# Strided attention on one core: moving the buffers of all transfers to multiples of 256 bytes in SBUF

## The chip, the cores and the metric

The kernel runs on one core of a Trainium2 chip. A core has a matrix engine (TensorE, PE in the profile), a vector engine (VectorE, DVE), an activation engine (ScalarE, ACT), a general engine (GpSimd, POOL) and a sync engine (SyncE, SP) that here does nothing but issue transfers. Sixteen DMA engines move data between the main memory (HBM) and the core's own memory (SBUF). SBUF has 128 partitions, and a tile takes the same range of bytes in each of them, so that a tile has one start address. PSUM is the small memory that TensorE writes. The metric is the time of one execution in microseconds; the kernel before takes 129.6 us (median of three runs, 129.14 to 129.7).

## The reference

Every query position attends to the same 16 key positions, those at multiples of 64. All data are float32; 8 batches times 12 heads make 96 heads of 1024 positions by 64 values.

```python
batch, heads, seq, dim = (8, 12, 1024, 64)      # stride 64
attend_positions = np.arange(0, seq, stride)
for i in range(seq):
    scores = np.einsum('bhqd,bhkd->bhqk', q, k) * scale     # k: K at the attended positions
    weights = np.exp(scores - np.max(scores, axis=-1, keepdims=True))
    weights = weights / (np.sum(weights, axis=-1, keepdims=True) + 1e-10)
    result[:, :, i, :] = np.einsum('bhqk,bhkd->bhqd', weights, v)[:, :, 0, :]
```

All of Q is read (25.2 MB) and all of the result written (25.2 MB); of K and V only 16 rows of each head are read, 0.4 MB each.

## The kernel before

The 96 heads are worked on in 24 groups of four, g = 0 to 23. A group's Q is 1 MB: one transfer loads it into one of ten buffers qn (QBUFS, lines 71 and 85), 8192 bytes in each partition. A group's result is 1 MB as well: it is gathered in one of eight buffers out_sb (OBUFS, lines 72 and 87) and one transfer stores it. K and V come at the start, each in one transfer of 256-byte rows, into k_raw and v_raw (lines 83, 84, 103 and 105).

For each group, `cast` (line 191) turns the loaded Q into bf16, one half on POOL and one on ACT; `transpose` (line 203) turns it on DVE; `scores` (line 213) multiplies it with the keys on PE in four matmuls into PSUM, and ACT takes the exponential; `values` (line 181) spreads the group's values on POOL; `outputs` (line 239) multiplies the weights with the values on PE, with the sums of the weights as further columns. DVE takes the reciprocals and scales two of the three parts of the result; ACT copies the third to SBUF and POOL scales it. `store` (line 265) writes the group out.

All transfers are issued on SP's queue by `_copy` (line 24), K and V by the queue's ordinary call. The order is written out by hand (line 80 switches the scheduler off): K, the first Q load, V and nine more Q loads at the start; then, in the loop over g from line 300, the steps ahead for later groups, the outputs of g, the store of g and the load of g + 10. The first two Q loads have rows of 8192 bytes on the side of the main memory (n = 128 in line 97), the others rows of 32768 bytes, each of which fills four partitions. A store reads 8192 bytes of each partition and writes them as two rows of 4096 bytes (line 269).

Every tile of the pool const (line 74) has its own place in SBUF, one behind the other in the order of the calls of const.tile. 16 KB and four small constants of 32 bytes each come first in SBUF, so the first tile, k_raw, begins at byte 16512. The two tiles that the change moves are identity (line 110, 256 bytes in each partition), from which the masks and the permutation are built at the start, and k_bf (line 141, 1536 bytes), the keys as bf16.

Of the kernel before, what the change touches and what calls it, by code (L numbers as in the profile page):

```python
# [10 lines left out]
FP32 = mybir.dt.float32  # L11
BF16 = mybir.dt.bfloat16
# [36 lines left out]
def kernel(  # L49
# [10 lines left out]
    B, H, S, D = Q.shape  # L60
# [3 lines left out]
    P = 128  # L64
    HG = 4
    NG = B * H // HG
    NC = NG // 2
# [6 lines left out]
    const = ctx.enter_context(tc.tile_pool(name="const", bufs=1))  # L74
# [5 lines left out]
    ctx.enter_context(tc.manual_schedule())  # L80


    k_raw = const.tile([P, NC, D], FP32, name="k_raw")
    v_raw = const.tile([P, NC, D], FP32, name="v_raw")
    qn_bufs = [const.tile([P, 32 * D], FP32, name=f"qn{i}") for i in range(QBUFS)]
    qb_bufs = [const.tile([P, 32 * D], BF16, name=f"qb{i}") for i in range(2)]
    out_bufs = [const.tile([P, 4, 8, D], FP32, name=f"out_sb{i}") for i in range(OBUFS)]
# [19 lines left out]
        load(g)  # L107


    identity = const.tile([P, P], BF16, name="identity")  # L110
    s_sel = const.tile([P, 4], BF16, name="s_sel")
    mask = const.tile([P, 4, D], BF16, name="mask")
    perm_v = const.tile([P, 2, 2, 2, 2, NK], BF16, name="perm_v")
# [24 lines left out]
    nc.gpsimd.tensor_copy(out=v_all[:, :, 4 * D :], in_=s_sel.unsqueeze(1).to_broadcast([P, 3, 4]))  # L138
    nc.gpsimd.tensor_copy(out=mask, in_=s_sel.unsqueeze(2).to_broadcast([P, 4, D]))

    k_bf = const.tile([P, NC, D], BF16, name="k_bf")
    k_r = const.tile([P, NC, D], BF16, name="k_r")
    v_bf = const.tile([P, NC, D], BF16, name="v_bf")
    v_rep = const.tile([P, NC, 2, D], BF16, name="v_rep")
# [205 lines left out]
```

## Time and profile before

| | |
|---|---|
| median of three runs | 129.6 us (129.14 to 129.7) |
| profiled execution | 129.29 us, its span 127.2 us |
| DVE, ACT, POOL, PE busy | 85.3, 84.6, 78.0, 62.8 us |
| data moved by DMA | 51.19 MB, mean 403 GB/s |
| Q loads, stores | 24 and 24 of 1 MB, median 14.5 and 14.4 us from issue to landing |

The span runs from the first to the last instruction of one profiled execution; the time of the execution has some 2 us more around it. Busy time is the sum of an engine's instructions. The page of the profile also cuts the span in 40 slices and gives the share of each in which an engine, and the 16 DMA engines on average, were busy. A packet is the piece in which a DMA engine moves data; the trace records the start, the length and the size of each.

### The profile page before, as it was taken

The page shows a single profiled execution, that of the slowest core. Times are in us where ns is not written, and L with a number is a line of the kernel's source. Part 1 is how long each engine was busy: PE and PEld are TensorE (multiplying, and loading weights), DVE is VectorE, ACT ScalarE, POOL GpSimd, SP SyncE. Part 2 cuts the span into 40 slices and gives each one's busy share as a digit, 9 for nine tenths or more (in the row PEclk, how much of TensorE's full clock was granted, in tenths as well). Part 3 has the DMA queues.
Part 4 walks back from the last instruction along what each step waited for, and adds up shares of the span by engine and source line. Part 5 has one row for each costly group of instructions (what it writes and reads, how often), then busy time and mean ns, then how long its engine had stood idle before and what let it go on. Part 6 is the DMA issues. An engine that isn't in the chain of part 4 may idle for free.

```text
span 127.2 us, 1113 instructions
## 1 busy us (share of the span) xinstructions
PE 62.8 (49%) x292; PEld 29.6 (23%) x292; DVE 85.3 (67%) x151; ACT 84.6 (66%) x111; POOL 78.0 (61%) x89
## 2 busy tenths in 40 slices
PE   0005259374656666667666646366777656420000
PEld 0001023132322332322333323133433323100000
DVE  5921385459967996796979799797987976730000
ACT  4171905968799989977897979979787895420000
POOL 4082365918567956897696997969689693451000
PEclk9999999959997799855999999999756999955555
DMA  2999999898998989999999989999999899999991
GB/s 65 360 320 492 423 402 454 371 474 340 505 407 369 513 348 417 461 379 438 461 384 443 477 363 469 430 387 492 402 387 484 363 420 430 425 420 430 425 410 59
DMA packets 7910, 51.19 MB, mean 403 GB/s; under 512 B 3872, under 2 KB 3872, under 8 KB 3872
## 3 DMA queue, kind: packets, MB, share of 16 engines
q1 hardware_dynamic: 7904, 51.12, 97.0%
q8 instruction: 2, 0.03, 0.1%
q14 instruction: 4, 0.03, 0.1%
HBM read 25.95 MB, written 25.17 MB: 402 GB/s over the span
## 4 chain that ended last, share of the span: by engine, by line
DVE 30%; POOL 18%; PE 15%; ACT 14%; DMA 7%; issue 4%; SPq 1%; POOLq 1%; DVEq 0%
DVE out_sb L256 15%; DVE qt L205 9%; POOL out_sb L259 8%; DMA qn<-in_Q_dram 7%; PE sc L218 7%; PE o_ps L246 6%; ACT out_sb L258 6%; POOL qb L195 5%; DVE rec L254 5%; POOL v_all L183 3%; ACT w_all L230 3%; ACT qb L196 2%; PE o_ps L170 1%; POOLq L345 1%; ACT k_t L158 1%
## 5 line engine op out<-in xcount | busy, mean ns | idle before, releaser
L246 PE MATMUL o_ps<-v_all,w_all 128*128 128x260 bf16 x192 | 37.0, 309 | 37.2 <-DVE out_sb L256 31.3
L259 POOL TENSOR_TENSOR out_sb<-out_sb,rec 128x768 f32<-128x768 f32 x24 | 35.3, 1471 | 27.2 <-ACT out_sb L258 27.2
L256 DVE TENSOR_TENSOR out_sb<-o_ps,rec 128x768 f32<-128x768 f32 (+1 forms) x48 | 39.6, 825 | 1.6
L230 ACT ACTIVATE w_all<-sc 64x512 bf16<-64x512 f32 x48 | 35.3, 735 | 5.2 <-PE sc L218 4.6
L205 DVE STREAM_TRANSPOSE qt<-qb 128x1024 int32<-128x1024 int32 x24 | 29.5, 1231 | 12.2 <-POOL qb L195 7.0
L218 PE MATMUL sc<-qt,k_t 128*128 128x512 bf16 x96 | 31.6, 462 | 10.2 <-DVE qt L205 10.2
L246 PEld LDWEIGHTS <-w_all 128*128 128x128 bf16 x192 | 18.5, 107 | 58.8 <-DVE out_sb L256 39.1
L258 ACT COPY out_sb<-o_ps 128x768 f32<-128x768 f32 x24 | 19.2, 798 | 17.4 <-DVE rec L254 17.1
L195 POOL CAST qb<-qn 128x1024 bf16<-128x1024 f32 x24 | 24.9, 1037 | 2.8 <-DMA qn<-in_Q_dram 2.8
L196 ACT CAST qb<-qn 128x1024 bf16<-128x1024 f32 x24 | 25.0, 1045 | 1.3 <-DMA qn<-in_Q_dram 0.7
L254 DVE RECIPROCAL rec<-o_ps 128x12 f32<-128x12 f32 (+1 forms) x72 | 15.1, 209 | 4.9 <-PE o_ps L246 4.5
L183 POOL TENSOR_TENSOR v_all<-mask,v_rep 128x256 bf16<-128x256 bf16 x24 | 16.0, 670 | 1.9 <-DVE v_rep L174 1.9
L218 PEld LDWEIGHTS <-k_t 128*128 128x128 bf16 x96 | 10.7, 111 | 20.3 <-POOL k_t L158 7.5
L174 DVE CAST v_rep<-o_ps 128x768 bf16<-128x768 f32 x2 | 1.9, 958 | 5.3 <-PE o_ps L170 5.3
L158 ACT COPY k_t<-k_r 32x256 bf16<-32x256 bf16 (+1 forms) x12 | 4.4, 366 | 1.1 <-DVE k_r L149 0.9
L131 DVE MEMSET k_t<- 128x3456 uint32 x1 | 2.9, 2938 | 1.5 <-PEq L331 1.5
L148 ACT CAST k_bf<-k_raw 128x256 bf16<-128x256 f32 (+1 forms) x2 | 1.0, 512 | 3.1 <-DMA k_raw<-in_K_dram 3.1
L138 POOL COPY v_all<-s_sel 128x12 bf16<-128x12 bf16 x1 | 0.2, 193 | 4.2 <-DVE s_sel L134 4.2
L170 PE MATMUL o_ps<-v_bf,perm_v 128*128 128x384 bf16 x4 | 1.6, 507 | 2.1 <-POOL v_bf L283 1.8
L148 ACT ACT_TABLE_LOAD x1 | 1.3, 1283 | 0.7 <-PEq L331 0.7
L149 DVE STREAM_TRANSPOSE k_r<-k_bf 128x128 int32<-128x128 int32 (+1 forms) x2 | 0.7, 370 | 1.4 <-ACT k_bf L148 1.4
L132 DVE MEMSET w_all<- 128x1536 uint32 x1 | 1.3, 1338 | 0.3 <-issue 0.3
(12 smaller groups left out, 4.6 us busy)
## 6 DMA issues: line engine op xcount, KB each, us to landing
qn<-in_Q_dram SPq DMA_DIRECT2D x24, 1024.0 KB, 14.5
out_dram<-out_sb SPq DMA_DIRECT2D x24, 1024.0 KB, 14.4
k_raw<-in_K_dram SPq DMA_DIRECT2D x1, 384.0 KB, 4.4
v_raw<-in_V_dram SPq DMA_DIRECT2D x1, 384.0 KB, 7.4
```

Of the source, the lines that this page charges most:

```text
L158: op(k_t[dst : dst + 32, 2 * part.start + c : 2 * part.stop : 2, :, col : col + NK], k_r[src : src + 32, part].rearrange("p n (a k f) -> p ...
L183: masked[g] = nc.gpsimd.tensor_tensor(out=vb[g][:, 0 : 4 * D].rearrange("p (s d) -> p s d", s=4), in0=mask, in1=v_rep[:, g // 2, g % 2].un ...
L195: nc.gpsimd.tensor_copy(out=qb[g][:, 0:half], in_=qn[g][:, 0:half]),
L196: nc.scalar.copy(qb[g][:, half:], qn[g][:, half:]),
L205: turned = nc.vector.transpose(qt[g].bitcast(I32), qb[g].bitcast(I32))
L218: nc.tensor.matmul(sc, lhsT=k_t[:, g, f, NK * (1 - e) : NK * (1 - e) + P], rhs=_ap_with(q, [q.ap[0], [D, 8], [16 * D, 2], [2, 32]], extra_ ...
L230: raised[g].append(nc.scalar.activation(out=_ap_with(wa, [wa.ap[0], [P, 8], [1, 2], [2, 32]], extra_offset=64 * a), in_=sc[64 * a : 64 * a ...
L246: nc.tensor.matmul(ps[:, i, 0 : 4 * D + 4], lhsT=wt[g][:, i0 + i], rhs=vb[g], start=True, stop=True,)
L254: nc.vector.reciprocal(r, ps[:, 0:n, 4 * D : 4 * D + 4])
L256: nc.vector.tensor_tensor(out=to, in0=o, in1=by, op=ALU.mult)
L258: copied = nc.scalar.copy(to, o)
L259: scaled[g] = nc.gpsimd.tensor_tensor(out=to, in0=to, in1=by, op=ALU.mult)
```

## The change

A tile edge of 32 float32 values, 128 bytes in each partition, is allocated ahead of all others, and nothing uses it. The tiles k_bf and identity are allocated right behind k_raw and v_raw instead of behind the output buffers. In the built program k_raw then begins at byte 16640, which is 65 times 256, v_raw at 19712 (77 times 256), the first Q buffer at 24576 (3 times 8192) and the first output buffer at 114688 (14 times 8192). Before, they began at 16512, 19584, 22656 and 112768. The instructions and their order on each engine are the same.

```diff
+    edge = const.tile([P, 32], FP32, name="edge")
     k_raw = const.tile([P, NC, D], FP32, name="k_raw")
     v_raw = const.tile([P, NC, D], FP32, name="v_raw")
+    k_bf = const.tile([P, NC, D], BF16, name="k_bf")
+    identity = const.tile([P, P], BF16, name="identity")
     qn_bufs = [const.tile([P, 32 * D], FP32, name=f"qn{i}") for i in range(QBUFS)]
     qb_bufs = [const.tile([P, 32 * D], BF16, name=f"qb{i}") for i in range(2)]
     out_bufs = [const.tile([P, 4, 8, D], FP32, name=f"out_sb{i}") for i in range(OBUFS)]
...
-    identity = const.tile([P, P], BF16, name="identity")
     s_sel = const.tile([P, 4], BF16, name="s_sel")
...
-    k_bf = const.tile([P, NC, D], BF16, name="k_bf")
     k_r = const.tile([P, NC, D], BF16, name="k_r")
```

## The prediction

> **What bounds the kernel now.** I read the page's slices first, then the table of DMA queues, then the waits of SP's queue and the timeline of the end, and last the DMA packets of single stretches. The slices and the queue table, from the page:
>
> ```profile
> DMA  2999999898998989999999989999999899999991
> GB/s 65 360 320 492 423 402 454 371 474 340 505 407 369 513 348 417 461 379 438 461 384 443 477 363 469 430 387 492 402 387 484 363 420 430 425 420 430 425 410 59
> ...
> q1 hardware_dynamic: 7904, 51.12, 97.0%
> ...
> qn<-in_Q_dram SPq DMA_DIRECT2D x24, 1024.0 KB, 14.5
> out_dram<-out_sb SPq DMA_DIRECT2D x24, 1024.0 KB, 14.4
> ```
>
> The 16 DMA engines are busy from the second slice to the last but one, and the packets of the one queue take 97.0% of 16 engines' span. A transfer of 1 MB needs about 2.5 us at 420 GB/s, yet lands 14.4 us after its issue: some six are queued at any time. No compute engine is over 67% busy.
>
> Does compute hold the DMA anywhere? The busy time by stretch (PE, PEld, DVE, ACT, POOL, then clock, DMA share, GB/s), the end of SP's timeline, and SP's own wait after its last issue:
>
> ```profile
> 14.00:24.00 10.00, 6.73 (x23) 2.59 (x21) 5.62 (x9) 5.17 (x7) 5.66 (x7) 1.00 1.00 419
> ...
> 75.00:90.00 15.00, 8.61 (x50) 4.44 (x51) 13.20 (x27) 13.11 (x17) 12.60 (x13) 1.00 1.01 427
> ...
> 114.00:124.00 10.00, 0.00 (x0) 0.00 (x0) 0.00 (x0) 0.00 (x0) 0.94 (x1) 0.50 1.00 419
> ```
> ```profile
> 111.98 3.53 SPq L33 DMA_DIRECT2D out_dram<-out_sb  x2
> ```
> ```profile
> SPq L345 <- DMA out_dram<-out_sb: 10.6, 2, 10.1
> ```
>
> The DMA share is 1.00 in stretches of loads alone (14 to 24 us), of both (75 to 90) and of stores alone (114 to 124). The last store is issued by 115.5 us; the kernel then only waits 10.6 us for packets. So a microsecond taken from or given to the packets' 16-engine time moves the end by a microsecond, and no compute wait matters until about 10 us were saved. The chain of waits on the page, full of DVE, ACT and POOL, is not what sets the end.
>
> **What a packet costs.** Three answers of the trace on DMA packets: the stores-only stretch (114 to 124 us), the loads-only stretch (14 to 24 us), and 0.34 us around one fetch of instructions (53.98 to 54.32 us):
>
> ```profile
> DMA packets 577, 4.19 MB, mean 419 GB/s; under 512 B 66, under 2 KB 66, under 8 KB 66
> ...
> q1 hardware_dynamic: 576, 4.18, 99.6%
> ```
> ```profile
> DMA packets 192, 4.19 MB, mean 419 GB/s; under 512 B 64, under 2 KB 64, under 8 KB 64
> ...
> q1 hardware_dynamic: 192, 4.19, 99.9%
> ```
> ```profile
> q14 instruction: 1, 0.01, 5.7%
> ```
>
> Stores: 0.996 x 16 x 10 us = 159.4 us, less 66 small packets of 9 ns, over 510 packets: 311 ns for 8192 bytes. Loads alone: (159.8 - 0.6) / 128 = 1244 ns for 32768 bytes; in the mixed stretches the packet records say 1218. The instruction fetch moves 8192 bytes and touches none of the kernel's tiles: 0.057 x 16 x 0.34 = 0.310 us (its record: 309 ns). The first two Q loads also go in packets of 8192 bytes, into buffers that lie 128 bytes past a multiple of 256; the commonest of their records is 309 ns as well. K and V go in 3072 packets of 256 bytes, nearly all 18 ns. All in all: 3072 store packets, 704 large and 256 small Q packets, 3072 of K and V, and 800 of 4 bytes (9 ns).
>
> **The change, part by part.**
>
> *Addresses.* In the built programs k_raw goes from byte 16512 to 16640, the Q buffers from 22656 + 8192 i to 24576 + 8192 i, the outputs from 112768 + 8192 i to 114688 + 8192 i. So before, every transfer began 128 bytes past a multiple of 256; afterwards none does. The buffers' distances from one another stay the same, and before, too, all of Q's and the outputs' shared one residue of 8192 (6272; now 0).
>
> *Instructions.* None is added, removed or moved on any engine or queue: k_bf and identity are only allocated earlier, edge is never touched. Engine operations read other columns of the same tiles; if any of them slowed, the 10.6 us of queued stores cover it. Cost 0.
>
> *Stores.* The bound from the nearest rows: 311 ns against 309 for the packet that touches no tile. If the 2 ns are the price of the odd start, 3072 x 2 / 16 = 0.38 us goes. They may as well belong to the two rows of 4096 bytes in which a store packet is written (the others go to one place). I take half, -0.2 us.
>
> *Q loads.* An odd start is hardly visible: 309 ns for the small ones, as without a tile, and 1218 for the large ones is less than 4 x 309 = 1236 although each fills four partitions' rows. Below: the large packets of the loads-only stretches lose their 26 ns, about 180 x 26 / 16 = -0.3 us. Above: the other 524 take what loads alone take, 524 x 26 / 16 = +0.85 us. I take 0, because the loads-only stretch differs by what runs beside it, not by its addresses.
>
> *K and V.* From 309 to 1218 ns a byte costs 909 / 24576 = 0.037 ns, so 256 bytes are 9.5 ns; with the 9 ns of a 4-byte packet that is 18.5 against 18 measured: nothing over. Below, all take the 15 ns that 161 of them took: 3072 x 3 / 16 = -0.6 us. I take 0.
>
> **Sum.** -0.2 us. The profiled execution took 129.29 us (span 127.2, 2.1 around it): it would take 129.1. It lies 0.3 under the median of the three runs, 129.6, which would be 129.4. A measurement of this kernel can tell about 0.5%, 0.65 us, from no change.
>
> **The rivals.**
>
> *An odd start costs the fetch of the 128 bytes before it, for reads of SBUF.* These are the stores. Price by rows: 128 x 0.037 = 4.7 ns of 311, x 3072 / 16 = -0.9 us: 128.7. For: the stores run at 419 to 428 GB/s with the engines full, so any waste inside a packet is time. Against: only 2 ns separate a store from a packet that touches no tile; the 4.7 would need some other part of the store to be shorter by 2.7.
>
> The Trainium skill has this rule (DMA: Bandwidth & Descriptors, section "How a descriptor splits into AXI transactions"): a transaction begins at a 256-byte boundary, and the bytes fetched ahead of an odd start are unused but cost beats. By that rule an 8192-byte read takes 260 beats instead of 256, an estimate of 1.5% on each store, which would also give about -0.9 us. The trace neither shows those beats nor excludes them.
>
> *The same on both sides.* Then a large load pays four times, 18.9 ns: 704 x 18.9 / 16 = 0.83 us; the small loads 0.08; K and V 3072 x 4.7 / 16 = 0.9; with the stores 2.7 us: 126.9. Against: the small loads at 309, and 256-byte packets whose 18 ns leave no room for 4.7.
>
> *Slower: buffers that all begin on a multiple of 8192 meet in one place of SBUF.* Every packet to or from a partition's row would then begin in the same columns of the memory, and streams that now pass each other would hinder each other, as loads do when alone (1244 instead of 1218). Price: the mixed loads 0.85 us: 130.4; if stores lengthened by the same 2%, 3072 x 6.5 / 16 = 1.2 more: 131.7. It decides from 0.65 x 16 / 3776 = 2.8 ns per large packet. Against: the buffers already shared one residue of 8192, so what meets what does not change, only where.
>
> *That the change does nothing* is close to my forecast: no row shows a cost of the odd start that is larger than 2 ns.
>
> **How the numbers follow.** Forecast, packets within 2 ns of what they are: 0.57, at 129.4, its own range 129.0 to 130.2. Reads alone cheaper: 0.20, at 128.7. Both sides: 0.09, at 126.9. Slower: 0.14, at 130.4 to 131.7. Faster by over 0.5% is the second and third, 0.29; within 0.5% the first, 0.57; slower 0.14. The range leaves out the third case and the upper half of the last: 127.9 to 130.8.
>
> **What would show it.** In the stores-only stretch the queue's share over its packet count, now 311 ns: 309 to 311 by the forecast, 306 by the first rival, 317 by the slower one. The large loads stay at 1218 beside stores and 1244 alone; 1199 would show the second rival. K and V stay at 18 ns. The last store's issue stays near 115 us with 10 to 11 us of packets behind it; if the time changes while all these stay, something outside the packets did it. The prediction is wrong if the overlap of successive packets, which a record does not show, hides a cost of the odd start that my comparison of record lengths misses.

## The result, and the profile after

The changed kernel takes 128.42 us (median of five runs, 128.40 to 128.64) against 129.53 us of the kernel before (129.14 to 129.70, five runs): 0.9924 of its time, 95% interval 0.9904 to 0.9944, some 1.0 us faster. In a second set of runs, beside other kernels, it was 0.9924 again (0.9911 to 0.9937). The time lies in the predicted range of 127.9 to 130.8, but not in the range of the case that was thought likeliest, 129.0 to 130.2: the change is faster by more than the 0.5% that a measurement can tell, which had a chance of 0.29.

The profiled execution took 128.42 us, its span 126.3 instead of 127.2. Slices and queue table of the page of the changed kernel:

```profile
DMA  2999989999998998979999989989989899999991
GB/s 63 371 345 467 498 374 457 436 394 384 449 496 340 490 426 363 511 327 441 454 392 433 470 376 462 465 361 490 423 369 501 353 423 418 428 433 420 420 423 67
...
q1 hardware_dynamic: 7904, 51.12, 97.0%
```

The same 7904 packets, the same bytes, and still 97.0% of a span that is 0.9 us shorter: the engines are as full as before and the packets took less time. SP's last wait, for the packets of the stores, in the changed kernel:

```profile
SPq L346 <- DMA out_dram<-out_sb: 9.5, 1, 9.5
```

It was 10.6 us; the DMA engines still have the last word, and nothing new waits. Adding up the packet records of the two traces by kind, over 16 engines, gives where the time came from:

| packets | before | after | gain |
|---|---|---|---|
| 3072 of K and V, 256 bytes | 3.54 us | 3.43 | 0.11 |
| 256 of the first two Q loads, 8192 bytes | 5.41 | 5.06 | 0.35 |
| 256 of the next eight Q loads, 32768 bytes | 19.89 | 19.53 | 0.36 |
| 448 of the later Q loads | 34.28 | 34.24 | 0.04 |
| 3072 of the stores | 59.80 | 59.73 | 0.06 |

With 0.01 from the packets of 4 bytes this is 0.93 us; the last packet ends at 124.98 instead of 125.86 us. Nearly all of it is gained in the first third, where loads run and stores don't. The loads-only stretch from 12 to 20 us shows it; the answers of the trace on its DMA packets, the kernel before and the changed one:

```profile
DMA packets 153, 3.44 MB, mean 430 GB/s; under 512 B 48, under 2 KB 48, under 8 KB 48
...
q1 hardware_dynamic: 153, 3.44, 102.4%
```
```profile
DMA packets 149, 3.28 MB, mean 410 GB/s; under 512 B 49, under 2 KB 49, under 8 KB 49
...
q1 hardware_dynamic: 149, 3.28, 95.1%
```

The rate and the share go by the packets that begin in the stretch, so with 1.2 us a packet they jump by 16 packets and are not to be compared; the time of one packet is. Before, (1.024 x 128 - 0.4) / 105 = 1244 ns; after, (0.951 x 128 - 0.4) / 100 = 1213 ns.

### The profile page after: what moved, and what is told of

It is laid out like the page before. It is cut to its first block, busy times and chain, and to the rows that moved or that the text cites. A ratio compares the mean times of both kernels' runs of the same rounds, so it can differ in the third digit from the quotient of the medians.

```text
span 126.3 us, 1113 instructions
## 1 busy us (share of the span) xinstructions
PE 64.3 (51%) x292; PEld 29.8 (24%) x292; DVE 85.8 (68%) x151; ACT 84.5 (67%) x111; POOL 78.1 (62%) x89
## 3 DMA queue, kind: packets, MB, share of 16 engines
q1 hardware_dynamic: 7904, 51.12, 97.0%
## 4 chain that ended last, share of the span: by engine, by line
DMA 37%; DVE 20%; ACT 11%; PE 9%; POOL 8%; issue 3%; SPq 1%; POOLq 1%; DVEq 0%
DMA qn<-in_Q_dram 37%; DVE out_sb L257 10%; DVE qt L206 6%; PE sc L219 4%; ACT out_sb L259 4%; PE o_ps L247 4%; POOL out_sb L260 3%; ACT w_all L231 3%; DVE rec L255 3%; ACT qb L197 3%; POOL qb L196 2%; POOL v_all L184 2%; POOLq L346 1%; DVE v_rep L175 1%; PE o_ps L171 1%
## 5 line engine op out<-in xcount | busy, mean ns | idle before, releaser
L247 PE MATMUL o_ps<-v_all,w_all 128*128 128x260 bf16 x192 | 38.3, 318 | 36.6 <-DVE out_sb L257 31.3
L219 PE MATMUL sc<-qt,k_t 128*128 128x512 bf16 x96 | 32.3, 470 | 9.9 <-DVE qt L206 9.9
L219 PEld LDWEIGHTS <-k_t 128*128 128x128 bf16 x96 | 10.6, 111 | 19.9 <-POOL k_t L159 7.5
```

What stands on the lines that cost most here:

```text
L219: nc.tensor.matmul(sc, lhsT=k_t[:, g, f, NK * (1 - e) : NK * (1 - e) + P], rhs=_ap_with(q, [q.ap[0], [D, 8], [16 * D, 2], [2, 32]], extra_ ...
L247: nc.tensor.matmul(ps[:, i, 0 : 4 * D + 4], lhsT=wt[g][:, i0 + i], rhs=vb[g], start=True, stop=True,)
```

## The experiments

My theory after the result: what pays for the odd start is the writing into SBUF, and only where loads run alone. Against it stood two others: that it is the reading by the stores (the first rival of the prediction), and that the multiples of 8192 matter rather than those of 256.

**The tile of 128 bytes alone.** k_bf and identity stay where they were, so that all transfers begin at odd multiples of 256.

```diff
+    edge = const.tile([P, 32], FP32, name="edge")
     k_raw = const.tile([P, NC, D], FP32, name="k_raw")
```

> Only the 128-byte tile is put first; k_bf and identity stay behind the outputs. K and V begin at 65 and 77 times 256, Q at 22784 = 89 times 256 and the outputs at 112896 = 441 times 256, neither a multiple of 512, still less of 8192. If a start at a multiple of 256 is all that counts: 1.0 us faster than before, as the changed kernel (0.992), large loads alone at 1213 ns. If multiples of 8192 count: within 0.2 us of before (1.000) and large loads alone at 1243 ns.

Measured: 128.16 us, 0.9899 of the kernel before (0.9881 to 0.9917); the commonest record of the large packets ahead of the stores is 1213 ns. It looked faster than the changed kernel by 0.26 us, so both were run on one chip:

> The kernel with the 128-byte tile alone (starts at odd multiples of 256) once more, on the same chip as the changed kernel. If it is really faster than the changed kernel: 128.1 to 128.2 us, 0.2 to 0.3 under it. If that was the chip of that run: within 0.1 us of it.

> The changed kernel as it is (Q and outputs at multiples of 8192), beside the one with the tile alone: 128.4 us if multiples of 8192 cost a little over multiples of 256, else the same as the other.

Measured: 128.56 us for the tile alone (0.9939, 0.9918 to 0.9959) and 128.36 for the changed kernel (0.9924, 0.9911 to 0.9937). The difference did not come back. Multiples of 256 give the gain; the moves of k_bf and identity add nothing that these runs can tell.

**One kind of transfer at a time.** Tiles of 128 bytes behind the ones shifted put the others back to an odd start.

```diff
 # kv_even
+    edge = const.tile([P, 32], FP32, name="edge")
     k_raw = const.tile([P, NC, D], FP32, name="k_raw")
     v_raw = const.tile([P, NC, D], FP32, name="v_raw")
+    gap = const.tile([P, 32], FP32, name="gap")
 # q_even
     v_raw = const.tile([P, NC, D], FP32, name="v_raw")
+    gap = const.tile([P, 32], FP32, name="gap")
...
     qb_bufs = [const.tile([P, 32 * D], BF16, name=f"qb{i}") for i in range(2)]
+    gap2 = const.tile([P, 32], FP32, name="gap2")
 # out_even
     qb_bufs = [const.tile([P, 32 * D], BF16, name=f"qb{i}") for i in range(2)]
+    gap2 = const.tile([P, 32], FP32, name="gap2")
```

> K and V begin at multiples of 256, Q and the outputs 128 bytes past one. If the gain comes from writes into SBUF, part of it from the 256-byte rows of K and V, whose backlog then holds up the first Q packets: 0.35 to 0.5 us faster (0.996 to 0.997), first Q packets of 8192 bytes at a mean of 316 to 320 ns instead of 338, large loads alone still at 1243. If the rows of K and V don't matter: 0 to 0.1 us, the first Q packets at 338.

> Only the Q buffers begin at multiples of 256. If writes into SBUF from an odd start are slower where loads run alone: 0.36 us faster plus what the first Q packets gain, 0.35 to 0.7 us together (0.995 to 0.997), large loads alone at 1213 ns. If reads of SBUF by the stores make the gain: 0 (1.000).

> Only the output buffers begin at multiples of 256. If reads from an odd start cost the bytes ahead of it: 0.9 us faster (0.993), stores at 306 ns. If only writes into SBUF matter: 0 to 0.1 us (0.999 to 1.000), stores at 311 ns.

Measured against 129.54 us of the kernel before: K and V 129.04 us (0.9958, 0.9942 to 0.9974), Q 128.59 (0.9927, 0.9907 to 0.9947), outputs 129.54 (1.0005, 0.9993 to 1.0016). So K and V give about 0.5 us, Q 0.95, the outputs nothing. The two gains add up to more than the whole change gave, by some 0.4 us; in the packet records of their profiled executions they are 0.54 and 0.56 us, against 0.93 for the whole. The 0.95 us of Q rests on four runs (0.69 to 1.20 by the interval) and is more than the 0.35 to 0.7 expected.

The stores-only stretch from 114 to 122 us shows that the stores did not change. Kernel before, then the one whose outputs alone begin at multiples of 256:

```profile
DMA packets 471, 3.40 MB, mean 425 GB/s; under 512 B 56, under 2 KB 56, under 8 KB 56
...
q1 hardware_dynamic: 470, 3.39, 101.1%
```
```profile
DMA packets 466, 3.40 MB, mean 425 GB/s; under 512 B 51, under 2 KB 51, under 8 KB 51
...
q1 hardware_dynamic: 465, 3.39, 101.1%
```

Both times 414 packets of 8192 bytes in the same share: 311 ns. The rival of the reads falls for this kernel.

What K and V do shows from 7 to 10 us, where V's last rows are followed by the packets of the second Q load, 8192 bytes each. Kernel before, Q alone even, K and V alone even:

```profile
DMA packets 1336, 1.04 MB, mean 345 GB/s; under 512 B 1248, under 2 KB 1248, under 8 KB 1248
```
```profile
DMA packets 1317, 1.07 MB, mean 357 GB/s; under 512 B 1224, under 2 KB 1224, under 8 KB 1224
```
```profile
DMA packets 1257, 1.20 MB, mean 399 GB/s; under 512 B 1146, under 2 KB 1146, under 8 KB 1146
```

With K and V even, the same 3 us move 1.20 MB instead of 1.04. The packet records say how: between 7 and 9 us 16 packets of 8192 bytes take over 500 ns, nearly all 547 to 575, in the kernel before, 14 with Q even, 16 with the outputs even, and none with K and V even, where they average 309 ns. That would be about one for each of the 16 engines, though the records do not name the engine. The rows of 256 bytes themselves got hardly shorter (18.4 to 17.8 ns on average); most of what their odd start costs falls on the packets behind them. That writes of theirs are still unfinished when the next packet comes would explain it, but is not shown.

What Q does shows in its large packets of 32768 bytes, ahead of the stores. Q alone even from 12 to 20 us, then K and V alone even from 14 to 24 us:

```profile
DMA packets 153, 3.44 MB, mean 430 GB/s; under 512 B 48, under 2 KB 48, under 8 KB 48
...
q1 hardware_dynamic: 153, 3.44, 100.3%
```
```profile
DMA packets 197, 4.36 MB, mean 436 GB/s; under 512 B 64, under 2 KB 64, under 8 KB 64
...
q1 hardware_dynamic: 197, 4.36, 103.5%
```

(1.003 x 128 - 0.4) / 105 = 1219 ns and (1.035 x 160 - 0.6) / 133 = 1241 ns, against 1244 in the kernel before. Q's start makes the difference, but neither kernel does quite what was expected. With Q alone even, the packet records show 1213 ns only for the first 16 large packets and 1216 to 1219 from then on. With K and V alone even, the first 58 took 1213 or 1214 ns, up to 14.2 us, although Q starts odd; from 16 us on they took 1240 to 1251. So the odd start does not lengthen every packet: the slow pace sets in after some time, and behind odd K and V, in the kernel before, it is there from the first large packet on.

**Loads by themselves, with four starts.** All but the loads and one store of the last buffer is taken out; a load waits for the one ten earlier into the same buffer.

```diff
-        n = P if g < 2 else 32
+        n = 32
...
+    for g in range(QBUFS):
+        load(g)
+    for g in range(QBUFS, NG):
+        load(g)
+    o = qn_bufs[(NG - 1) % QBUFS]
+    _copy(
+        nc,
+        _ap_with(out, [[16 * D, P], [2 * SD, 2], [1, 16 * D]], (NG - 1) * HG * SD),
+        _ap_with(o, [o.ap[0], [1, 1], [1, 32 * D]]),
+    )
```

An edge of 0, 128, 192 or 160 bytes ahead of the tiles sets the start of Q to 128, 0, 64 or 32 bytes past a multiple of 256.

> Nothing but the 24 loads of Q, all in packets of 32768 bytes, and one store of the last buffer: all computation, K, V and the other 23 stores are left out. Q begins 128 bytes past a multiple of 256. If writes into SBUF run at the pace seen in the loads-only stretch of the kernel before: packets at 1240 to 1246 ns, 768 packets x 1238 / 16 = 59.4 us of packets.

> The same loads, Q at a multiple of 256. If the start alone makes the difference: packets at 1213 ns and 768 x 27 / 16 = 1.3 us less than with the start 128 bytes past. If the loads-only stretch was slow for another reason (K and V ahead of it, engines that read the buffers): less than 0.3 us apart.

> The same loads, Q 64 bytes past a multiple of 256. If what costs is that a row of 8192 bytes touches one stretch of 256 bytes more, however little of it: as 128 bytes past, 1.3 us over the even start. If multiples of 64 bytes are enough: as the even start. If the cost goes with the bytes past the boundary: half, 0.65 us.

> The same loads, Q 32 bytes past a multiple of 256. One stretch more: 1.3 us over the even start. Bytes past the boundary: a quarter, 0.3 us. Multiples of 32 enough: 0; multiples of 64 needed: more than 64 bytes past costs.

| start past a multiple of 256 | time | range |
|---|---|---|
| 0 | 68.70 us | 68.65 to 68.72 |
| 32 bytes | 69.92 | 69.87 to 69.95 |
| 64 bytes | 69.99 | 69.96 to 70.09 |
| 128 bytes | 69.99 | 69.93 to 70.10 |

The even start is 1.29 us faster than 128 bytes past, where 1.3 was expected. The DMA packets from 20 to 40 us, 128 bytes past and even:

```profile
DMA packets 388, 8.45 MB, mean 423 GB/s; under 512 B 130, under 2 KB 130, under 8 KB 130
...
q1 hardware_dynamic: 388, 8.45, 100.7%
```
```profile
DMA packets 386, 8.42 MB, mean 421 GB/s; under 512 B 129, under 2 KB 129, under 8 KB 129
...
q1 hardware_dynamic: 386, 8.42, 98.1%
```

(1.007 x 320 - 1.2) / 258 = 1244 ns a packet against (0.981 x 320 - 1.2) / 257 = 1217. No computation and no K or V is there, and the one store begins after 63 us, so the 27 ns belong to the start alone. Of the 1.29 us, 1.15 lie in the loads, whose last large packet begins at 60.23 instead of 61.38 us; the rest comes with the store behind them. And 32 bytes past cost nearly what 128 do. The cost does not go with the bytes past the boundary; it goes with there being an odd start at all, as it would if a row that touches one stretch of 256 bytes more took one step more. A packet writes four such rows, so an estimate of the price is 27 / 4 = 6.7 ns a row. No run shows the step itself, and here too the pace is not there at once: from the odd start the packets that begin between 7.4 and 10.0 us took 1213 to 1216 ns, those from 11 us on 1240 to 1251; from the even start most took 1213 ns until some 22 us, and from 26 us on 1218 or 1219. Writes that fall behind the reads until something is full would look like this; what it is stays open.

**Stores by themselves.** The eight output buffers are set to 1, then all 24 stores go out.

```diff
+    for o in out_bufs:
+        nc.vector.memset(o, 1.0)
...
+    for g in range(NG):
+        out_sb[g] = out_bufs[g % OBUFS]
+        store(g)
```

> Nothing but the 24 stores, from output buffers set to 1 beforehand: loads and all computation are left out. The outputs begin 128 bytes past a multiple of 256. Packets at 311 ns as in the stores-only stretch of the kernel before, 3072 x 307 / 16 = 59 us of packets.

> The same stores from output buffers at multiples of 256. If reads from an odd start fetch the bytes ahead of it and that sets the pace of stores: 0.9 us less than with the start 128 bytes past, packets at 306 ns. If only writes into SBUF pay: within 0.1 us, packets at 311 ns.

Measured: 67.66 us (67.65 to 67.69) from the odd start and 66.50 (66.49 to 66.51) from the even one, 1.16 us apart. This I had not expected, nor that the packets from the odd start would take more than 311 ns. From 20 to 40 us, odd, then even:

```profile
DMA packets 1149, 8.36 MB, mean 418 GB/s; under 512 B 128, under 2 KB 128, under 8 KB 128
...
q1 hardware_dynamic: 1149, 8.36, 101.7%
```
```profile
DMA packets 1164, 8.49 MB, mean 424 GB/s; under 512 B 128, under 2 KB 128, under 8 KB 128
...
q1 hardware_dynamic: 1164, 8.49, 100.9%
```

(1.017 x 320 - 1.2) / 1021 = 318 ns against (1.009 x 320 - 1.2) / 1036 = 311. Over the whole run the records average 316.2 and 309.9 ns, and from the odd start they scatter from 309 to over 320, while from the even one 2434 of 3072 are 309. So reads of SBUF from an odd start can cost as well, 6.3 ns a packet; but the stores at the end of the full kernel, which run as alone as these and from the same odd addresses, take 311 ns from either start. Why they are spared is not settled by these runs.

## Why the prediction was right and where it was wrong

- **What bounds the kernel** held: packet time saved came out at the end. The packets of the profiled executions lost 0.93 us, the span 0.89, the execution 0.87 (129.29 to 128.42), and SP still waits 9.5 us for the last stores.
- **Instructions cost nothing** held: DVE, ACT and POOL are busy for 85.8, 84.5 and 78.1 us, as before within 0.5 us.
- **Its signs:** only the large loads alone moved, from 1244 to 1213 ns. The stores stayed at 311 ns, K and V at 18 in the commonest record, and the last store is issued by 115.75 us instead of 115.5. The time lies in the range by luck: what reached down to 127.9 was the rival of the reads, whose mechanism gave nothing here, and the loads that made the gain stood in the sum as 0.
- **Stores, -0.2 us:** -0.06 by the records, and 1.0005 of the time when they alone are moved. The 2 ns between 309 and 311 don't belong to the start.
- **Q loads, taken as 0:** this step failed. The prediction named the loads-only stretch and gave the 26 ns of its large packets as the lower bound, -0.3 us, but took 0 "because the loads-only stretch differs by what runs beside it, not by its addresses". The addresses were it: the large packets ahead of the stores, 256 and not some 180, gave 0.36 us, and loads by themselves show the 27 ns with nothing else running. The comparison with the packets of 309 ns misled, because it took the commonest record of packets of 8192 bytes at the very start, where a delay falls on a few others.
- **K and V, taken as 0:** failed too, and the list of terms lacked the larger part. Their own packets gave 0.11 us. The first Q packets gave 0.35, mostly because the long ones behind V's rows went away (0.30 with K and V alone even); the prediction looked at the commonest record of these packets, 309 ns, and not at their mean, 338.
- **The first rival, reads alone, at 128.7,** gives nearly the right time for the wrong reason: the outputs alone gained nothing in this kernel. The Trainium skill's rule (DMA: Bandwidth & Descriptors, section "How a descriptor splits into AXI transactions") speaks of bytes fetched ahead of an odd start. Where stores ran by themselves, 1.16 us agrees with its direction and roughly with the 0.9 us estimated from it; in the full kernel the trace does not show it. Of bytes wasted in writes that section says nothing; in the loads by themselves 32 and 128 bytes past cost 1.22 and 1.29 us, so the number of bytes past the boundary is not what counts there.
- **The second rival, both sides, at 126.9,** had the right side for the loads but the wrong extent: beside stores the large packets average 1224 ns from the odd start and 1223 from the even one, so two thirds of them gain next to nothing. That writing which lags behind is made up while a store's packets read would explain this; it was not tested by itself.
- **Slower through multiples of 8192:** not seen. The tile alone and the whole change can't be told apart.

## What to carry to other kernels

Where the DMA engines set the end, look at the start addresses of the buffers: here a single unused tile of 128 bytes at the front of the pool gave 1.0 and 0.6% in two sets of runs, where the whole change gave 0.8%. In this kernel the cost of an odd start sat where loads ran alone, at the start, and part of it fell on packets behind the ones that caused it. So compare mean packet times by stretch and kind, not the commonest record, and when a row is slow only in one stretch, ask whether the stretch merely uncovers a cost that is hidden elsewhere.

## What the runs showed of the hardware that was not expected

- Writes into SBUF by loads alone: 1244 ns for 32768 bytes when each partition's row begins 32, 64 or 128 bytes past a multiple of 256, 1213 to 1219 ns when it begins on one. The slow pace sets in late: with K and V alone even, the first 58 such packets took 1213 or 1214 ns from the odd start too. Beside stores the means are 1224 and 1223 ns.
- Rows of 256 bytes that begin 128 bytes past a multiple delay the packets behind them: in the kernel before, 16 packets of 8192 bytes took 547 to 575 ns behind V's rows, and none there took over 500 once K and V began at multiples of 256.
- Stores by themselves: 316.2 ns for 8192 bytes read from an odd start, 309.9 from an even one, while the stores at the end of the full kernel take 311 from both. This difference stays open.
